# A two-layer backbone kernel on one core: the conditioning vector's silu behind the first tiles, the last tile's root on ScalarE, and another order of all steps

## Chip, cores and metric

The kernel runs on one core of one Trainium2 chip. The metric is device time in microseconds (us), the median over runs; smaller is better. The core has TensorE (PE, matmuls; its weight loads are shown apart as PEld), VectorE (DVE), ScalarE (ACT), GpSimd (POOL) and SyncE (SP), which here only issues transfers (DMA). All data are in fp32; a matmul in the profile works on 128 rows by 256 or 512 columns.

## What is computed

Two layers over 512 latent tokens of width 1024, with 256 context tokens in layer 0. Cut to what matters here:

```python
silu_c = jax.nn.silu(c); silu_cc = jax.nn.silu(c_ctx)
for i in range(2):
    mod_l = silu_c @ ada_w[i] + ada_b[i]                 # six vectors: shifts, scales, gates
    mod_c = silu_cc @ ada_w[i] + ada_b[i]
    h = modulate(rmsnorm(x, norm_g[i, 0]), shift, scale)
    y = mixer(h)                                         # layer 0: windowed attention, layer 1: gated MLP
    x = x + gate * rmsnorm(y, norm_g[i, 1])
    f = swiglu(modulate(rmsnorm(x, norm_g[i, 2]), shift2, scale2), ffn_w_in[i], ffn_w_out[i])
    x = x + gate2 * rmsnorm(f, norm_g[i, 3])
return x
# rmsnorm(y, g) = y * rsqrt(mean(y*y) + 1e-6) * g
```

## The kernel before, in words

**Numbers.** Each fp32 operand is split into a high part, rounded on ACT (`high`, L412, a CAST), and a low part, the difference, on DVE (`low`, L419). A product is then three matmuls: high by high, high by low, low by high. So each slab of weights that comes in costs one CAST and one subtraction before PE may use it whole.

**Order.** The program is a list of steps. `at(time, step, ...)` puts a step on a plan with a due time, but a table of names at the head of the file, `ORDER`, overrides the time: `run_plan` emits the steps in the table's order. Each engine gets its instructions in that order and works them off one by one, waiting at each for what it needs. SP's queue and POOL's queue issue the transfers in the same way. So ORDER decides, for every engine, what stands behind what.

**Start.** The conditioning vector `cc` is loaded by the first transfer, outside the plan; ACT takes its silu (L547) into `sc`, and DVE spreads it into `s4` (L650). Six tiles of tokens (`xin`, four of x and two of ctx) are fetched; for each, ACT takes the mean square (L439), DVE adds the epsilon and POOL raises to -0.5 (`rstd_of`, L448/449), DVE scales (L676), and PE transposes it in two groups of four (`turn_in`, L697). The layer's first modulation vectors come in eight pieces of weights (`ada0`, 1 MB each), which PE multiplies with `s4` (`ada0_rows`, L718) and turns (L729). Then `kv` (L471 to 473) is the first product, over eight slices of the width. `warm` (L684) are matmuls on zeros, to keep PE running while data come. `rope` (L915) turns the tables of the rotary embedding.

**Middle.** Queries and keys are rotated; the last key halves' low parts (`klo`) are needed by the first score (L1099). Later modulation vectors are summed on DVE from chunks and added up over partitions by a matmul with ones (`total`, L612), whose operand is split first (`acc_st`).

**FFN.** For each layer, 22 hidden blocks are formed (L1635), with fewer products by a Strassen-like scheme. The output side is a second such scheme: after the first plain products (`plain7`, L1846, tiles of two banks each) come seven block products (`product7`, L1819), numbered 1 to 7, each in four parts p. Block product i, part p needs the cast weights (`w7_high_i_p`, an ACT CAST), their low part on DVE and cast tokens (`a7_high_i_p`, ACT CAST into `s`). The weights of the blocks (11, 12, 21, 22) are fetched by SP into `w`/`t` tiles (`fetch7_z_h`), and the sums of two blocks are made either on DVE (`t7`, L1801) or by a transfer that POOL issues and that adds in flight (`t7_add`, L1807). Results are saved (`save7`, L1827) and combined (`add7`, L1836).

**End.** In layer 1 the last plain products (`plain7_9`, `plain7_10`) finish the four tiles of the output, y00/y01 for tile 0 to y30/y31 for tile 3. For each tile: `square_y` on ACT for each half (L439), `rstd_y` (DVE L448, POOL L449), `gain_y` on DVE (L1319), `add_x` on DVE (L1323), `store` on SP. Tile 3 is done in halves, each half with its own squares, gains, addition and store. In the old table its second half's matmuls are the very last.

Of the kernel before, what the change touches and what calls it, by code (L numbers as in the profile page):

```python
# [46 lines left out]
ada0_fetch_1 dma#2 ada0_fetch_2 ada0_fetch_4 square_in_2 turn_in_0_0 ada0_rows_out_0 turn_in_0_1 rstd_in_2 norm_in_2_0
norm_in_2_1 ada0_cols_0 turn_in_2_0 whigh_0_0 ada0_rows_1 rope_turned_0 turn_in_2_1 turned_in_0_0 ada0_rows_out_1
turn_in_3_0 <lambda> ada0_done_0 modulate0_ctx_0 ada0_cols_1 wlow_0_0 modulated_ctx_0 kv_0_4 kv_0_5 turned_in_2_0
ada0_done_1 turned_in_3_0 modulate0_0 modulated_high_0 modulated_low_0 wfetch_0_1 modulated_high_1 ada0_rows_2  # L50
ada0_rows_out_2 kv_0_2 turned_in_2_1 modulate0_ctx_1 modulate0_1 modulated_ctx_1 ada0_cols_2 kv_0_1 whigh_0_1 kv_0_0
modulated_low_1 kv_1_4 kv_1_1 kv_1_2 kv_1_5 ada0_done_2 ada0_fetch_3 rope_turned_1 modulate0_ctx_2 turned_in_0_1
modulate0_2 m2start wlow_0_1 modulated_high_2 ada0_rows_4 modulated_ctx_2 ada0_rows_3 ada0_rows_out_4 ada0_cols_4
ada0_done_4 kv_1_0 ada0_rows_out_3 ada0_cols_3 wfetch_1 whigh_1_0 wlow_1_0 whigh_1_1 kv_2_4 modulated_low_2 kv_0_3
ada0_fetch_5 kv_1_3 kv_2_3 kv_2_1 ada0_done_3 modulate0_3 modulated_high_3 modulate0_ctx_3 ada0_rows_5 modulated_ctx_3
kv_3_4 kv_2_5 kv_3_5 modulate0_ctx_4 modulated_ctx_4 modulated_high_4 kv_2_2 kv_4_5 kv_2_0 modulated_low_3
ada0_rows_out_5 ada0_cols_5 kv_3_2 kv_3_3 m2fetch_0 m2add_0 kv_3_0 kv_3_1 dma#3 ada0_fetch_6 ada0_rows_6 m2add_1
modulate0_4 <lambda>#2 ada0_done_5 modulated_high_5 modulate0_ctx_5 ada0_fetch_7 ada0_rows_7 modulated_low_4 kv_4_2
wfetch_2 kv_4_3 ada0_rows_out_6 ada0_cols_6 wlow_1_1 modulate0_5 modulated_low_5 whigh_2_0 wlow_2_0 ada0_done_6
modulate0_6 kv_4_4 ada0_rows_out_7 kv_4_0 m2fetch_1 m2add_2 m2add_3 modulated_high_6 modulated_low_6 kv_5_0 q_first_0_0  # L60
kv_5_3 whigh_2_1 ada0_cols_7 dma#4 modulated_ctx_5 ada0_done_7 modulated_high_7 wlow_2_1 modulate0_ctx_6 kv_4_1 kv_5_1
q_first_0_1 q_first_0_2 q_first_0_3 q_first_0_4 q_first_0_5 kv_5_2 kv_6_3 kv_5_5 modulate0_7 modulated_ctx_6 q_first_0_6
kv_6_0 kv_5_4 m2fetch_2 modulated_low_7 modulate0_ctx_7 kv_7_3 kv_6_1 m2add_4 kv_6_4 m2add_5 m2fetch_3 kv_6_2 kv_7_2
wfetch_3 kv_6_5 kv_7_0 q_first_0_7 kv_7_1 modulated_ctx_7 m2add_6 m2add_7 kv_7_5 kv_7_4 q_first_1_0 table_Exp k_copy_2_0
k_copy_2_1 q_rows_0 v_copy_0 k_copy_0_0 k_rope_2 k_add_2 k_copy_0_1 v_copy_1 k_copy_4_0 k_copy_4_1 v_copy_2 k_rope_0
v_copy_3 q_first_1_1 q_first_1_2 q_first_1_3 q_first_1_4 q_first_1_5 q_first_1_6 q_first_1_7 k_turn_2_1 k_add_0 v_copy_4
# [2167 lines left out]
```

## Time and profile before

| | us |
|---|---|
| median of 3 runs | 1097.65 (1097.63 to 1099.7) |
| the profiled execution | 1098.59 |
| its span | 1096.8 |
| PE busy | 1077.8 |
| DVE busy | 939.1 |
| ACT busy | 601.0 |
| POOL busy | 263.1 |

Rows of the profile give a line of the program, an engine, an operation, and names "out<-in" without their numbers. In a row of waits, "PE y L1819 <- ACT s L412: 1.3, 1, 1.3" means that PE stood idle ahead of a matmul of line 1819 into `y` until ACT's instruction of line 412 on `s` was done, 1.3 us in all, once, at most 1.3. In a timeline, the first two columns are start and duration, and a bracket gives the idle time before and what ended it. In a row of windows come the stretch, its length, the busy time and number of instructions of PE, PEld, DVE, ACT and POOL, PE's granted clock, the share of DMA engines' time and GB/s. The mean granted clock of TensorE was 0.999 of full speed.

### The profile page before, as it was taken

Reading aid. Unit: us, or ns where it says so; the run is one execution under the profiler, and the core shown is the slowest. Engines: PE = TensorE matmul, PEld = TensorE weight load, DVE = VectorE, ACT = ScalarE, POOL = GpSimd, SP = SyncE. Lnnn points to the kernel's source line nnn. Section 1 sums busy time; section 2 is a strip of 40 time slices with the busy share of each in tenths; the row PEclk is TensorE's granted clock in tenths of the full one; section 3 lists DMA queues with packets and bytes.
Section 4 is the critical chain, followed back from the end, with each engine's and each line's share of the span. In section 5 each row is a group of like instructions: output and inputs, shape, how many; then the busy total and the mean of one; then the engine's idle time right before and its main releaser. Section 6 shows DMA issues by size and latency. Waiting matters only on the chain.

```text
span 1096.8 us, 17794 instructions
## 1 busy us (share of the span) xinstructions
PE 1077.8 (98%) x6894; PEld 948.3 (86%) x6894; DVE 939.1 (86%) x1382; ACT 601.0 (55%) x1055; POOL 263.1 (24%) x268
## 2 busy tenths in 40 slices
PE   8999999999999999999899999999999999999997
PEld 5787787878999999998688888888999999998886
DVE  5788998848999999998788878878998888879885
ACT  6456677656554555546565534336655555556662
POOL 1428768426500000003311402006300000003301
PEclk9999999999999999999999999999999999999999
DMA  9745531254245636569942586561233344369911
GB/s 357 285 153 169 179 109 46 78 188 177 77 174 192 212 117 196 170 213 248 238 88 78 203 271 236 192 197 73 96 134 120 113 154 143 113 229 315 172 28 77
DMA packets 50392, 181.25 MB, mean 165 GB/s; under 512 B 5370, under 2 KB 9722, under 8 KB 39172
## 3 DMA queue, kind: packets, MB, share of 16 engines
q1 hardware_dynamic: 42756, 165.44, 43.7%
q0 software_dynamic: 7552, 14.68, 7.9%
q8 instruction: 54, 0.88, 0.3%
q14 instruction: 30, 0.25, 0.1%
HBM read 171.71 MB, written 2.10 MB: 158 GB/s over the span
## 4 chain that ended last, share of the span: by engine, by line
PE 89%; DVE 5%; DMA 3%; issue 1%; ACT 1%; SPq 0%; DVEq 0%; POOLq 0%; POOL 0%; ACTq 0%
PE f L1635 36%; PE y L1819 12%; PE y L479 7%; PE y L1846 6%; PE v L479 4%; PE s_ps L1099 2%; PE pT_ps L1132 2%; PE o_ps L1148 2%; PE q_ps L861 1%; DMA t<-in_w 1%; PE fa L471 1%; PE fa L473 1%; PE fa L472 1%; PE u L2054 1%; PE u L2053 1%; PE u L2052 1%
## 5 line engine op out<-in xcount | busy, mean ns | idle before, releaser
L1635 PE MATMUL f<-H,w_hi 128*128 128x256 f32 x960 | 177.8, 284 | 0.5 <-DVE fc L1646 0.5
L1635 PEld LDWEIGHTS f<-H,w_hi 128*128 128x128 f32 x960 | 150.0, 192 | 1.3 <-DVE fc L1646 1.0
L1635 PE MATMUL f<-H,w_lo 128*128 128x256 f32 x480 | 135.8, 283 | 0.0
L1819 PE MATMUL y<-w_hi,s 128*128 128x512 f32 x448 | 120.6, 390 | 2.5 <-ACT s L412 1.3
L1635 PE MATMUL f<-S,w_hi 128*128 128x256 f32 x640 | 118.5, 284 | 0.5 <-ACT fc L1642 0.5
L412 ACT CAST w_hi<-T 128x1024 fp32r<-128x1024 f32 x80 | 83.7, 1047 | 58.7 <-PE f L1635 41.5
L412 ACT CAST w_hi<-w_raw 128x1024 fp32r<-128x1024 f32 x90 | 94.0, 1054 | 31.1 <-PE f L1635 11.3
L1819 PEld LDWEIGHTS y<-w_hi,s 128*128 128x128 f32 x448 | 83.9, 188 | 20.8 <-DVE s L419 1.8
L419 DVE TENSOR_TENSOR w_lo<-w_raw,w_hi 128x1024 fp32r<-128x1024 f32 (+1 forms) x81 | 96.1, 1192 | 6.4 <-ACT w_hi L412 6.1
L1635 PEld LDWEIGHTS f<-S,w_hi 128*128 128x128 f32 x640 | 99.8, 192 | 0.9 <-ACT fc L1642 0.7
L419 DVE TENSOR_TENSOR w_lo<-T,w_hi 128x1024 fp32r<-128x1024 f32 x80 | 97.3, 1219 | 2.6 <-ACT w_hi L412 2.6
L1635 PEld LDWEIGHTS f<-H,w_lo 128*128 128x128 f32 x480 | 92.1, 192 | 0.0
L1635 PE MATMUL f<-S,w_lo 128*128 128x256 f32 x320 | 90.6, 283 | 0.0
L1642 ACT COPY fc<-f 128x256 f32<-128x256 f32 x120 | 43.6, 372 | 84.2 <-PE f L1635 75.6
L1807 POOL DMA_DIRECT2D t<-in_w x48 | 42.5, 955 | 178.3 <-DMA t<-in_w 105.1
L581 DVE SCALAR_TENSOR_TENSOR acc<-ada_k,sc,acc 128x1024 f32<-128x1024 f32 x56 | 71.6, 1278 | 6.1 <-DMA ada_k<-in_ada 5.7
L595 POOL DMA_DIRECT2D acc<-acc x8 | 6.9, 868 | 286.2 <-DVE acc L581 279.1
L1819 PE MATMUL y<-w_lo,s 128*128 128x512 f32 x224 | 69.3, 391 | 1.1 <-DVE w_lo L419 1.1
L1126 POOL TENSOR_SCALAR p<-p,st 128x512 f32<-128x512 f32 (+1 forms) x64 | 59.8, 948 | 27.5 <-DVE st L1122 14.5
L1635 PE MATMUL f<-H,x 128*128 128x256 f32 x480 | 64.1, 283 | 0.0
L1110 ACT ACTIVATE p<-s_ps,st 128x512 f32<-128x512 f32 (+1 forms) x64 | 47.3, 741 | 25.9 <-DVE st L1105 22.3
L1635 PEld LDWEIGHTS f<-S,w_lo 128*128 128x128 f32 x320 | 61.4, 192 | 0.0
(261 smaller groups left out, 2746.4 us busy)
## 6 DMA issues: line engine op xcount, KB each, us to landing
w_raw<-in_w SPq DMA_DIRECT2D x67, 1024.0 KB, 5.4
ada_k<-in_ada SPq DMA_DIRECT2D x56, 512.0 KB, 5.9
ada_raw<-in_ada SPq DMA_DIRECT2D x12, 1024.0 KB, 5.4
w<-in_w SPq DMA_DIRECT2D x12, 1024.0 KB, 7.6
t<-in_w POOLq DMA_DIRECT2D x48, 256.0 KB, 6.3
ada<-in_ada SPq DMA_DIRECT2D x8, 1024.0 KB, 8.4
t<-in_w SPq DMA_DIRECT2D x8, 1024.0 KB, 10.7
w_raw<-in_w SPq DMA_DIRECT2D x10, 512.0 KB, 7.3
```

The lines of the kernel that those rows point to most:

```text
L412: nc.scalar.copy(out=hi, in_=src)
L419: (eng or nc.vector).tensor_tensor(out=v(lo), in0=v(src), in1=v(hi).bitcast(F32), op=ALU.subtract)
L479: nc.tensor.matmul(dst, l, w[:, n * 512:(n + 1) * 512], start=first and i == 0, stop=last and i == 2)
L581: nc.vector.scalar_tensor_tensor(out=self.acc, in0=self.raws.pop(k), scalar=sc[:, k:k + 1], in1=self.acc, op0=ALU.mult, op1=ALU.add)
L1099: nc.tensor.matmul(dst, q, keys, start=i == 0, stop=i == 1)
L1110: nc.scalar.activation(out=p[:, 0:self.n], in_=self.s[j], func=AF.Exp, scale=-1.0, bias=self.st[:, 4 + j:5 + j], accum_out=self.st[:, 8 + ...
L1126: nc.gpsimd.tensor_scalar(out=p, in0=p, scalar1=self.st[:, 12 + j:13 + j], scalar2=1.0, op0=ALU.mult, op1=ALU.mult)
L1635: nc.tensor.matmul(dst, l[:, w], r[:, k, :], start=first and k == 0 and j == 0, stop=k == 3 and j == 2, skip_group_check=True)
L1642: nc.scalar.copy(out=self.c[n][:, i * 256:(i + 1) * 256], in_=self.ps[n, 1 if i == 1 else 0])
L1807: nc.gpsimd.dma_start(out=self.tt[:, p * D + 512 * i:p * D + 512 * (i + 1)], in_=a["w"][F2[self.layer] + 1 + 2 * p + i][:, c:c + 512], acc ...
L1819: nc.tensor.matmul(self.bank7(i, j), st[:, c:c + P], w[:, z * 512:(z + 1) * 512], start=i == 1 and p == 0 and l == 0 and z == 0, stop=p == ...
L1846: nc.tensor.matmul(self.y[t][n], st[:, x + t * P:x + (t + 1) * P], parts[h][w][:, n * 512:(n + 1) * 512], start=v == 0 and h == 0 and i == ...
```

## The change

Three things. First, the transfer of `cc`, its silu and its spread become steps `cc_in`, `cc_silu` and `cc_spread` of the plan, and the table sets their places. Second, in the last stage the tile that is done in halves (tile 3) gets its inverse root otherwise: DVE adds the epsilon to the first half's mean square (`bias_y`), ACT takes the root of the second half's with that as its bias (`root_y`, Sqrt) and DVE inverts (`invert_y`); the root's table is loaded ahead, by `table("Sqrt")`, and `table` now takes minus the constant as its operand so that a root of it exists. Third, ORDER is another list throughout; of its old and new names only those steps differ.

```diff
-x_fetch_1 square_in_1 rstd_in_1 norm_in_1_0 rope_in warm_0 warm_1 warm_2 warm_3 norm_in_1_1 x_fetch_4 square_in_4
+rope_in dma rope_turn_0 rope_turned_0 x_fetch_3 warm_0 warm_1 warm_2 warm_3 square_in_3 rstd_in_3 warm_4 norm_in_3_1
...
     def table(func):
-        nc.scalar.activation(out=tabled, in_=mhalf, func=getattr(AF, func))
+        nc.scalar.activation(out=tabled, in_=mhalf, func=getattr(AF, func), scale=-1.0)
...
-    dma(cc, a["cc"])
...
-    nc.scalar.activation(out=sc, in_=cc, func=AF.Silu)
...
-    for z in range(2):
-        nc.vector.tensor_copy(out=s4[:, :, 2 * z], in_=sc[:, z * KC:(z + 1) * KC])
+    def cc_in():
+        dma(cc, a["cc"])
+    def cc_silu():
+        nc.scalar.activation(out=sc, in_=cc, func=AF.Silu)
+    def cc_spread():
+        for z in range(2):
+            nc.vector.tensor_copy(out=s4[:, :, 2 * z], in_=sc[:, z * KC:(z + 1) * KC])
...
     at(0, x_fetch, 0)
+    at(.1, cc_in)
+    at(4, cc_silu)
+    at(4.2, cc_spread)
...
+        def bias_y(self):
+            self.b = small(1, "by")
+            nc.vector.tensor_scalar(out=self.b, in0=self.ms[0], scalar1=RMS_EPS, scalar2=None, op0=ALU.add)
+        def root_y(self):
+            self.r = small(1, "ry")
+            nc.scalar.activation(out=self.r, in_=self.ms[1], func=AF.Sqrt, bias=self.b)
+        def invert_y(self):
+            nc.vector.reciprocal(out=self.r, in_=self.r)
...
-                at(e + .15, c.rstd_y)
+                at(e + .05, c.bias_y)
+                at(e + .12, c.root_y)
+                at(e + .15, c.invert_y)
+            at(b, table, "Sqrt")
```

**Start.** ACT's instructions at the program's head, before (`sc<-cc` is the silu; `xin` are the tiles, in the order in which they are taken: x1, ctx4, x3, ctx5, x0):

```order
L551 ACT_TABLE_LOAD
L551 CAST ones_73<-ones32_71 128x128
L547 ACT_TABLE_LOAD
L547 ACTIVATE sc_69<-cc_61 128x16
L439 ACTIVATE junk_108,ms0_107<-xin_105 128x1024
L439 ACTIVATE junk_125,ms0_124<-xin_122 128x1024
L439 ACTIVATE junk_135,ms0_134<-xin_132 128x1024
L703 COPY xnT0_97<-xT_141 128x4x128
L439 ACTIVATE junk_168,ms0_167<-xin_146 128x1024
```

and after (the tiles are x3, ctx5, x1, ctx4, x0):

```order
L551 ACT_TABLE_LOAD
L551 CAST ones_71<-ones32_69 128x128
L930 COPY ropeT_83<-rope_104 128x512
L441 ACTIVATE junk_130,ms0_129<-xin_122 128x1024
L441 ACTIVATE junk_150,ms0_149<-xin_147 128x1024
L654 ACT_TABLE_LOAD
L654 ACTIVATE sc_68<-cc_61 128x16
L441 ACTIVATE junk_165,ms0_164<-xin_162 128x1024
L441 ACTIVATE junk_187,ms0_186<-xin_184 128x1024
```

The silu and its table load have moved from ahead of all tiles to behind the squares of two of them. On SP the order of fetches has changed with it: rope, ident, x3, cc, ctx5, x1, cols, ctx4, x0, x2, and then the first piece of `ada0`; x2 came behind that piece before. On PE all twelve groups of transposes now stand ahead of the `rows` of the second piece; two stood behind it.

**Layer 0's seven products.** ACT's instructions around the weights of product 2, parts 2 and 3, before (`w_hi_5909` and `w_hi_5914` are the weights of product 7, parts 3 and 2, `w_hi_5920` and `w_hi_5926` those of product 2, parts 3 and 2; `s7_5929` are the tokens of 2_2):

```order
L412 CAST w_hi_5909<-t7_5724 128x1024
L412 CAST s7_5912<-act4_5055 128x512
L412 CAST w_hi_5914<-t7_5724 128x1024
L412 CAST s7_5918<-act4_4430 128x512
L412 CAST w_hi_5920<-t7_5724 128x1024
L412 CAST w_hi_5926<-t7_5724 128x1024
L412 CAST s7_5929<-act4_4430 128x512
```

and after (`w_hi_5948` and `w_hi_5953` are product 7, parts 2 and 3, `w_hi_5958` and `w_hi_5978` product 2, parts 2 and 3; `s7_5951` are the tokens of 2_2, `s7_5975` those of 2_3):

```order
L414 CAST w_hi_5948<-t7_5694 128x1024
L414 CAST s7_5951<-act4_4447 128x512
L414 CAST w_hi_5953<-t7_5694 128x1024
L414 CAST w_hi_5958<-t7_5694 128x1024
L414 CAST s7_5975<-act4_4976 128x512
L414 CAST w_hi_5978<-t7_5694 128x1024
```

The tokens of 2_2 now come ahead of its weights, and its weights ahead of those of 2_3. On SP the fetch of these weights (`fetch7_21_1`) keeps its place behind `fetch7_22_0_raw`, which waits for the step `t7_3` of DVE as before. On PE product 2_2 is still the eleventh of the parts. In layer 1 the table moves `f1fetch7_12_1_raw` from ahead of blocks 12, 21 and 22 to behind both halves of 22, and the sums `f1t7_2` and `f1t7_3` that need it to just ahead of product 5.

**End.** ACT's last instructions before (y31 is the second half of tile 3, y10 and y11 are tile 1):

```order
L439 ACTIVATE junk_11194,msy_11193<-y01_10503 128x512
L439 ACTIVATE junk_11197,msy_11196<-y00_10502 128x512
L439 ACTIVATE junk_11212,msy_11211<-y20_10433 128x512
L439 ACTIVATE junk_11227,msy_11226<-y21_10434 128x512
L439 ACTIVATE junk_11254,msy_11253<-y30_10468 128x512
L439 ACTIVATE junk_11270,msy_11269<-y10_10527 128x512
L439 ACTIVATE junk_11273,msy_11272<-y11_10528 128x512
L439 ACTIVATE junk_11297,msy_11296<-y31_10469 128x512
```

and after:

```order
L441 ACTIVATE junk_11196,msy_11195<-y30_10518 128x512
L441 ACTIVATE junk_11205,msy_11204<-y31_10519 128x512
L1332 ACTIVATE ry_11211<-msy_11204,by_11209 128x1
L441 ACTIVATE junk_11234,msy_11233<-y20_10488 128x512
L441 ACTIVATE junk_11237,msy_11236<-y21_10489 128x512
L441 ACTIVATE junk_11255,msy_11254<-y01_10470 128x512
L441 ACTIVATE junk_11258,msy_11257<-y00_10469 128x512
L441 ACTIVATE junk_11295,msy_11294<-y10_10453 128x512
L441 ACTIVATE junk_11301,msy_11300<-y11_10454 128x512
```

Tile 3, with the root on ACT (L1332), now comes first of the four, and tile 1 last; PE's last 24 matmuls are those of y10 and y11 in turn, where the last 12 were those of y31 alone. The last two stores are whole tiles of 512 KB, where they were halves of 256 KB. DVE's sum `add7_c12_1` into y11, which PE's last matmuls need, stands behind the gains, the inversion and an addition of tile 3 and the gains of tile 2.

More of the change, by code (lines that the diff above doesn't have):

```diff
@@ L47 @@
[L47 to L66, printed above, removed]
@@ new lines @@
+c1turned_hi_0 c3merge c2rstd_x c3square_y c3gain_y c3rstd_y f0part_high_2_0 c1turned_lo_0 f0first_half_1#2
+f0part_low_2_0 c3add_x c3gain_x c2shift_x_1 f0head_0_2 c1turned_hi_1 f0head_1_0 c1turned_lo_1 c3square_x c2turn_1
+c3rstd_x f0part_high_3_0 c2shift_x_0 c2turned_hi_1 m5start c3shift_x_0 f0head_1_1 f0diff_2_1 f0first_half_0
+f0part_high_2_2 m5fetch_chunk_1_spare m0fetch_gain c2turn_0 c3shift_x_1 c2turned_hi_0 c2turned_lo_0 f0diff_2_3
+f0diff_2_2 f0part_low_3_0 f0sum_a_S3 f0product_2_1 c2turned_lo_1 c3turn_1 f0part_low_2_2 f0sum_a_S2 f0first_half_0#2
@@ new lines @@
+f0keep_12_2 f0product_13_1 f0up2_11 f0keep_12_1 f0part_high_13_1 f0part_high_13_2 m0fetch_chunk_3_spare f0gate1_11
+f0silu_11_0 f0keep_13_0 f0product_12_3 f0product_11_4 f0silu_11_1 f0gate1_12 m0add_chunk_2 f0part_low_13_1
+f0part_low_13_2 f0gates_11 m5stack f0part_high_14_0 f0part_high_14_2 f0product_13_5 f0diff_14_1 f0part_low_14_0
+wfetch_25 f0product_12_7 f0up2_12 m1fetch_chunk_0_spare f0part_high_13_3 f0diff_14_3 f0diff_14_2 f0part_low_13_3
+f0product_13_6 f0keep_13_1 f0product_13_2 f0product_12_4 f0keep_13_2 f0product_13_7 f0up1_12 m5total_0_slot
@@ new lines @@
+f0plain7_0_2 f0plain7_0_3 f0t7_2 f0save7_v0_0 f0save7_v0_1 f0a7_high_1_0 f0gates_21 m1total_0_slot f0a7_high_2_1
+m1done_512 m1done_0 f0w7_low_1_0 f0w7_high_1_1 f0a7_low_2_1 f0fetch7_12_1 f0s7_S3_1 f0fetch7_21_0 f0a7_low_1_0
+f0w7_low_1_1 f0a7_high_1_1 f0a7_low_1_1 f0plain7_0_1 f0a7_high_1_2 f0w7_high_1_2 f0t7_add_1_22 f0plain7_0_0
+f0a7_high_1_3 f0w7_high_2_1 f0w7_low_1_2 f0w7_high_2_0 f0a7_high_2_0 f0a7_low_1_2 f0product7_1_0 f0a7_high_7_1
+f0product7_1_1 f0t7_add_0_22 f0t7_0 f0w7_low_2_0 f0product7_1_2 f0a7_low_1_3 f0w7_high_7_0 f0s7_S3_2 f0t7_3
@@ new lines @@
+whigh_48_1 m4fetch_chunk_1 wlow_47_1 u_part_0_1 v_part_3_(3,) v1rstd v0mean wlow_48_1 wlow_48_0 m4fetch_chunk_2
+m4add_chunk_1 m4add_chunk_2 table_Gelu v0var v0rstd v0gain v1gain m4fetch_chunk_5 v0bias v3add v1bias wfetch_49
+whigh_49_0 u_part_1_0 m4fetch_chunk_4 m2mirror#2 m4add_chunk_3 v3gelu v3mean v2add v3var whigh_49_1 wfetch_50
+m4add_chunk_4 wlow_49_0 m4add_chunk_5 v2gelu v2mean v2var m4fetch_chunk_7 u_part_1_1 m4fetch_chunk_6 wlow_49_1
+u_part_2_0 whigh_50_0 whigh_50_1 wlow_50_1 m3fetch_chunk_0 ws_in wfetch_51 m3start#2 bias_in m2stack#2 v2rstd
@@ new lines @@
+f1keep_16_2 f1part_high_17_0 f1part_low_17_0 f1diff_17_3 f1diff_17_2 f1part_high_17_2 gains f1part_low_17_2
+f1product_16_2 f1product_16_7 f1up2_16 f1silu_13_1 f1product_17_1 f1product_16_3 f1keep_17_0 f1part_high_17_1 f1gates_13
+f1product_15_7 f1product_17_2 f1diff_18_1 f1diff_17_4 wfetch_74 f1part_high_18_0 f1up2_15 f1silu_15_0 f1product_15_4
+f1silu_15_1 f1product_16_4 m5add_chunk_5#2 f1part_high_17_3 f1part_low_17_1 f1up1_16 f1product_17_5 f1keep_17_1
+f1s7_S3_2 f1gate1_17 f1gate1_16 f1product_17_6 f1silu_16_0 f1diff_18_3 f1diff_18_2 f1diff_18_4 f1part_high_18_2
@@ L395 @@
+c2add_x#4 c0gain_y_0_512 c0gain_y_512_1024 f1plain7_9_1 c0rstd_y#4 c0add_x#4 c0store f1plain7_10_1 c3add_x_0_512
+c1square_y_0_512 c1gain_y_0_512 c3store_0_512 c1square_y_512_1024 c1rstd_y#4 c1gain_y_512_1024 c2store c1add_x#4 c1store
 """.split()
```

659 lines of the change are left out of this document (327 added, 332 removed).

## The prediction

> **What bounds the kernel now.** I read the page first, for the share of each engine.
>
> ```profile
> PE 1077.8 (98%) x6894; PEld 948.3 (86%) x6894; DVE 939.1 (86%) x1382; ACT 601.0 (55%) x1055; POOL 263.1 (24%) x268
> ```
>
> TensorE (PE) is busy for 1077.8 of 1096.8 us. The change adds and removes no matmul, so all that it can win lies in the 19.0 us in which PE does nothing. The waits of PE say what these are:
>
> ```profile
> PE warm L684 <- DVE idle L681: 1.8, 1, 1.8
> PE xT L697 <- DVE r L446: 1.6, 1, 1.6
> PE y L1819 <- ACT s L412: 1.3, 1, 1.3
> PE s_ps L1099 <- DVE klo L419: 1.2, 1, 1.2
> PE y L1819 <- DVE s L419: 1.2, 1, 1.2
> PE xT L697 <- DVE xin L676: 1.2, 2, 0.7
> PE y L1819 <- DVE w_lo L419: 1.1, 1, 1.1
> PE s_ps L1099 <- ACT p L1110: 1.0, 2, 0.7
> PE f L1635 <- DVE fc L1646: 0.5, 1, 0.5
> PE f L1635 <- ACT fc L1642: 0.5, 1, 0.5
> ```
>
> The rows of L684 and L697 (1.8, 1.6 and 1.2) lie ahead of the first product and cost nothing by themselves, as the chain of the first 24 us shows:
>
> ```profile
> 2.13 5.61 DMA xin<-in_ctx
> 7.74 0.02 issue
> 7.76 12.80 DMA ada<-in_ada
> 20.69 1.07 PE rows L718 x16
> 21.76 1.02 PE xT L697 x8
> ```
>
> There transfers set the pace, and PE begins the `rows` of the second piece of the modulation weights at 20.69, when that piece is in. From then on PE hardly stops before its last matmul. The rest of the idle time is in three places: four waits of about 1.2 us each from the list above, smaller ones, and the end after the last matmul. So I look at the start, at those waits, and at the end, each against the new order of its engine.
>
> **The start.** The change puts the load of `cc` fourth on SyncE's queue, and Silu with its table load behind two tiles' squares on ScalarE (ACT). What these cost ACT is in its timeline:
>
> ```profile
> 2.35 1.28 ACT L547 ACT_TABLE_LOAD   x1
> 3.64 0.22 ACT L547 ACTIVATE sc<-cc 128x16 f32<-128x16 f32 x1
> 5.01 1.06 ACT L439 ACTIVATE junk<-xin 128x1024 bf16<-128x1024 f32 x1 [1.15 <-DMA xin<-in_x]
> 7.83 1.06 ACT L439 ACTIVATE junk<-xin 128x1024 bf16<-128x1024 f32 x1 [1.67 <-DMA xin<-in_ctx]
> 16.55 1.07 ACT L439 ACTIVATE junk<-xin 128x1024 bf16<-128x1024 f32 x1
> ```
>
> Before, load and Silu (1.28 + 0.22 = 1.50 us) lay in the time ACT waits for its first tile, which came in at 5.0. After, they stand between squares, while ACT waited 1.67 for the third tile anyway; so the 1.5 us have a cover of 1.15 + 1.67 in all, and I put them at nothing. If that cover is gone (the tiles come closer together), they delay all later squares by up to 1.5. The last tile's square was at 16.55 because the tile came late; in the new order of fetches this tile comes ahead of the first piece of weights. Two of the twelve groups of transposes stood behind `rows` before: the row "21.76 1.02 PE xT L697 x8". In the new order of PE all twelve groups precede that `rows`, and the bytes queued ahead of the second piece are the same, so it lands as before. The first product then begins one group of transposes earlier: **-1.0 us**. Bounds: -1.6 if PE's earlier wait on `r` (1.6) vanishes as well and shifts the pieces, +0.5 if the 1.5 us of load and Silu hit with 1.0 saved. I take -1.0, the row itself.
>
> [...]
>
> **The first scores (83 us).** PE waits 1.2 for `klo` once. DVE's timeline has the subtractions for it:
>
> ```profile
> 83.06 1.28 DVE L419 TENSOR_TENSOR klo<-kT,khi 128x512 fp32r<-128x512 f32 x2
> ```
>
> The first score reads what the second of the two writes. In the new order the two have changed places, and one takes 1.28 / 2 = 0.64, so **-0.6**; bounds 0 and -1.2, the whole wait.
>
> **The modulation totals (485 to 488 us).** PE's timeline:
>
> ```profile
> 487.75 0.50 PE L612 MATMUL ada_ps<-acc_st,ones 128*128 128x512 f32 x1 [0.28 <-ACT acc_st L412]
> 488.48 0.50 PE L612 MATMUL ada_ps<-acc_st,ones 128*128 128x512 f32 x1 [0.23 <-DVE acc_st L419]
> ```
>
> With the wait of `f` on `fc` (0.5) just ahead, these are 0.28 + 0.23 + 0.5 = 1.0 us. The new order takes the first total earlier, among the products of the last hidden block, and the second later, inside the plain product; both operands have then been cast for long. I take **-0.8**, between 0 and -1.0.
>
> **The seven products of layer 0 (533 to 541 us).** ACT's timeline and PE's:
>
> ```profile
> 532.24 1.99 ACT L412 CAST w_hi<-t 128x1024 fp32r<-128x1024 f32 x2 [8.02 <-DMA t<-in_w]
> 534.14 1.13 ACT L412 CAST s<-act 128x512 fp32r<-128x512 f32 x2
> ```
>
> ```profile
> 534.81 0.73 PE L1819 MATMUL y<-w_hi,s 128*128 128x512 f32 x2 [1.32 <-ACT s L412]
> 536.67 0.74 PE L1819 MATMUL y<-w_lo,s 128*128 128x512 f32 x2 [1.13 <-DVE w_lo L419]
> 541.35 0.50 PE L1819 MATMUL y<-w_hi,s 128*128 128x512 f32 x1 [1.17 <-DVE s L419]
> ```
>
> ACT stands 8.02 us at a cast whose weights are not yet in, with the cast of the tokens `s` behind it. When they come, at 532.2, it does two weight casts (1.99) before that `s` (1.13 for two), and PE, whose queue has run dry, loses 1.32 + 1.13 + 1.17 = 3.6. The fetch stands at the same place in SyncE's queue after, behind the same step of DVE, so I let it land at the same time. But ACT's order is another: the tokens of product 2_2 are cast ahead of the wait, and the weights of 2_2 ahead of those of 2_3. Left over is then one weight cast and one subtraction for its low part, which PE sees as one wait like that of 1.13 (1.2 with a margin): 3.6 - 1.2 = **-2.4**. Bounds: 0 if the other pieces come in later and the wait only changes its name, -3.6 if all goes.
>
> **The end.** Here the change of the last tile's root lies. The old end:
>
> ```profile
> 1087.67 0.39 PE L1846 MATMUL y<-w_lo,st 128*128 128x512 f32 x1
> 1089.94 0.39 PE L1846 MATMUL y<-w_hi,st 128*128 128x512 f32 x1
> ```
>
> ```profile
> 1090.42 0.60 ACT L439 ACTIVATE junk<-y 128x512 bf16<-128x512 f32 x1 [1.54 <-PE y L1846]
> ```
>
> ```profile
> 1088.92 0.22 DVE L448 TENSOR_SCALAR ry<-msy 128x1 f32<-128x1 f32 x1
> 1089.83 1.28 DVE L1323 SCALAR_TENSOR_TENSOR x<-tmp,ry,x 128x1024 f32<-128x1024 f32 x1
> 1092.02 1.41 DVE L1323 SCALAR_TENSOR_TENSOR x<-tmp,ry,x 128x512 f32<-128x512 f32 x2
> ```
>
> ```profile
> 1091.44 0.55 POOL L449 TENSOR_TENSOR ry<-ry,mhalf 128x1 f32<-128x1 f32 x1 [1.68 <-DVE ry L448]
> ```
>
> PE ends at 1089.94 + 0.39 = 1090.33. One square, the addition of the epsilon, the power on GpSimd (POOL, 0.55) and two half additions (1.41) follow, until 1092.02 + 1.41 = 1093.43, that is 3.10 after PE; the last store holds 256 KB, since the first half left ahead of it. Sending the root to ACT shortens this chain by the way to POOL and back, if this tile is the last. But in the new order of PE the split tile, tile 3, with the new root, is the first of the four to end; tiles 2 and 0 follow, and the last 24 matmuls are those of tile 1, on two banks in turn, with the old chain. What that costs is shown by tile 1 in the old run: its last matmul lay 12 matmuls ahead of the end, at the pace of (1089.94 - 1087.67) / 10 = 0.227 us, so at 1090.33 - 2.73 = 1087.60; its addition ended at 1089.83 + 1.28 = 1091.11, 3.51 after it, since two squares follow each other instead of one. That is +0.4 against 3.10. Its store is one of 512 KB:
>
> ```profile
> 12.00:20.00 8.00, 6.42 (x56) 4.93 (x57) 6.34 (x15) 5.82 (x12) 2.72 (x4) 1.00 1.02 417
> ```
>
> At the 417 GB/s that the DMA engines moved in this window when full, 256 KB more take 0.6. Together +1.0 us, and I add 0.2, since the sum that DVE must write into `y11` ahead of its last matmuls now stands behind the gains and the first half addition of tile 3: **+1.2**. Bounds +0.6 (stores overlap fully but for half of the second square) and +1.9 (PE waits a whole 0.69 addition more). So the new root itself, 0.55 us of power taken away, wins nothing at the end: no engine waits for it there. Its table load lies in a stretch in which ACT is idle for half of the time:
>
> ```profile
> 1040.00:1085.00 45.00, 45.00 (x199) 36.77 (x198) 34.60 (x46) 21.12 (x32) 4.36 (x5) 1.00 0.16 30
> ```
>
> ACT is busy 21.12 of 45.00 us there, so 1.28 are free; if it hit just when PE needs a cast, it would cost up to 1.28.
>
> **What the rest of the order brings.** Every engine's order differs nearly everywhere, and the trace can't show the waits that it makes. The list above is what an order leaves between 23 and 1090 us: ten or so waits, from 0.5 to 1.3. I allow **+0.7** for new ones, between 0 and 3.6, the largest cluster that the old order left.
>
> **Sum.** -1.0 - 0.6 - 0.8 - 2.4 + 1.2 + 0.7 = -2.9. The profiled run took 1098.59 us (span 1096.8), so it would be 1095.7 there; the median of the runs before is 1097.65, 0.94 lower, which makes 1094.8. A measurement can tell some 0.2% (2.2 us) of this kernel from no change, so "faster" begins below 1095.45 and "slower" above 1099.85.
>
> **Rivals.** *The wait in layer 0 keeps its size.* PE's wait at 533 to 541 is at bottom a transfer that lands at 532; if weights land no earlier and 2_2 is as late by its low part and the next tokens, the -2.4 falls away: -2.9 + 2.4 = -0.5, 1097.15. For it speaks that the fetch stands where it stood; against it that the first of the three waits is on `s`, which is now cast ahead. Chance 0.27.
>
> *Slower: the same stall comes again in layer 1.* There the new order fetches the second half of block 12 last, behind both halves of block 22, and DVE's sums of it with block 11 stand directly ahead of product 5 that uses them. If that transfer lands after PE's queue of product 3 has run dry, ACT stands at the cast as in the row of 8.02 and PE loses another 3.6, while layer 0 keeps its own: -0.5 + 3.6 = +3.1, 1100.75. It decides when the transfer lands later than PE's products 1, 7, 2, 6 and 3 last. Against it: PE had no such wait in layer 1 before, and the DMA share is low there (0.16 in the window above). Chance 0.15.
>
> *The Silu becomes the bound of the start.* If the tiles come in close together, the 1.50 us lie on the chain of squares and the start gives +0.5 instead of -1.0: -2.9 + 1.5 = -1.4, 1096.25. Chance 0.10. [...]
>
> *The new order is better than I can see.* All four gains at their bounds (-1.6 - 1.2 - 1.0 - 3.6), the end at +1.0 and no new waits: -6.4, 1091.25. Chance 0.10.
>
> That the change does nothing of what its name says for the last tile is not a rival but part of the forecast: by the order it isn't last.
>
> **How the numbers follow.** The forecast has 0.38, and by its unknown waits reaches from 1093 to 1096.5; of this 0.31 is faster and 0.07 the same. The better order adds 0.10 to faster, the kept wait 0.03 faster, 0.21 same, 0.03 slower, the Silu 0.02 faster and 0.08 same, the stall in layer 1 0.15 slower. Faster 0.46, same 0.36, slower 0.18. The range from 1091.0 to 1100.5 takes in forecast and both cases of no change, and cuts the two ends about in the middle.
>
> **What would show it.** Right: the first product begins near 21.7 to 22; PE's waits on `s` at 533 to 541 shrink to one of about 1.2; PE ends about 4 us earlier against the span's start than 1090.33, and the span ends 7.4 to 7.7 after PE instead of 6.5, with a 512 KB store last. Wrong: a wait of PE above 2 us at a new place, a first product later than 23, or a tail of 6 us or less.

## The result and the profile after

The changed kernel is slower: 1101.18 us in the median of 8 runs (1099.49 to 1102.26) beside 1097.82 for the kernel before (8 runs, the three of the table above among them, 1097.63 to 1099.7); ratio 1.0028, 95% interval 1.0018 to 1.0037. 1094.8 was forecast. Its profiled run took 1101.11, span 1099.3, that is 2.5 us more than the 1096.8 of before.

The first row of the page, and all rows of the waits of PE that the changed kernel has:

```profile
PE 1078.4 (98%) x6894; PEld 950.6 (86%) x6894; DVE 941.6 (86%) x1383; ACT 601.9 (55%) x1058; POOL 264.7 (24%) x267
```

```profile
PE q_ps L872 <- DVE klo L421: 7.5, 1, 7.5
PE rope L926 <- DMA ident<-in_ident: 3.6, 1, 3.6
PE s_ps L1110 <- ACT p L1121: 2.0, 3, 1.0
PE pT_ps L1143 <- ACT pt L1150: 0.2, 1, 0.2
```

Read against the list of before: every wait on which the prediction put a gain is gone, those of `y` (1.3, 1.2 and 1.1), of `f` (0.5 and 0.5), of `ada_ps` (0.3 and 0.2) and that of the first score on `klo`. The scores wait longer for `p` (2.0 instead of 1.0); the wait of `rope` lies ahead of the `warm` matmuls and costs nothing by itself. In place of those that are gone stands one of 7.5 us, which the list of before has not: PE's third query product, `q_ps`, waits for a subtraction of keys on DVE, with which it shares no operand. PE's and DVE's timelines at that place:

```profile
73.32 2.78 PE L1030 MATMUL kT<-ident,kr 128*128 128x128 f32 x24
83.58 1.22 PE L872 MATMUL q_ps<-HA,w_hi 128*128 128x512 f32 x2 [7.47 <-DVE klo L421]
84.60 0.63 PE L872 MATMUL q_ps<-HA,w_lo 128*128 128x512 f32 x1
...
87.56 0.63 PE L872 MATMUL q_ps<-HA,w_hi 128*128 128x512 f32 x2
...
91.00 0.39 PE L1110 MATMUL s_ps<-khi,q_X 128*128 128x512 f32 x1
```

```profile
76.13 1.28 DVE L421 TENSOR_TENSOR klo<-kT,khi 128x512 fp32r<-128x512 f32 x2
81.04 1.28 DVE L421 TENSOR_TENSOR klo<-kT,khi 128x512 fp32r<-128x512 f32 x2
82.84 1.28 DVE L421 TENSOR_TENSOR klo<-kT,khi 128x512 fp32r<-128x512 f32 x2
```

The product begins at 83.58, when the first subtraction of the third pair has ended (82.84 + 0.64 = 83.48). In the kernel before, the same product followed the transposes at once. PE's rows and one of DVE's:

```profile
74.74 2.78 PE L1019 MATMUL kT<-ident,kr 128*128 128x128 f32 x24
77.56 0.73 PE L861 MATMUL q_ps<-HA,w_hi 128*128 128x512 f32 x2
78.13 0.39 PE L861 MATMUL q_ps<-HA,w_lo 128*128 128x512 f32 x1
...
84.49 0.47 PE L1099 MATMUL s_ps<-khi,q_X 128*128 128x512 f32 x1 [1.19 <-DVE klo L419]
```

```profile
76.83 0.68 DVE L419 TENSOR_TENSOR klo<-kT,khi 128x512 fp32r<-128x512 f32 x1
```

There is a second loss in these rows. After the pause the 24 matmuls of the product take 91.00 - 83.58 = 7.42 us; at 0.227 each they would take 5.45. The first nine come 0.44 apart ((87.56 - 83.58) / 9), the rest 0.23. The pause so costs 7.5 and another 2.0. The granted clock shows the second part: it is half from 80.69, within the pause, until 87.51 (rows of windows):

```profile
80.69:84.10 3.41, 0.52 (x1) 0.50 (x2) 3.41 (x6) 1.12 (x2) 1.95 (x3) 0.50 0.62 154
84.10:87.51 3.41, 3.41 (x9) 2.64 (x8) 1.39 (x3) 0.11 (x1) 0.00 (x0) 0.50 0.00 0
87.51:90.92 3.41, 3.41 (x16) 2.77 (x15) 0.00 (x0) 0.00 (x0) 0.00 (x0) 1.00 0.00 0
```

The end of the changed kernel, on PE and DVE:

```profile
1091.24 0.61 PE L1868 MATMUL y<-w_hi,st 128*128 128x512 f32 x2
```

```profile
1092.45 0.69 DVE L1341 TENSOR_TENSOR tmp<-y,row 128x512 f32<-128x512 f32 x1 [0.46 <-ACT junk L441]
1093.17 0.22 DVE L450 TENSOR_SCALAR ry<-msy 128x1 f32<-128x1 f32 x1
1094.09 1.28 DVE L1345 SCALAR_TENSOR_TENSOR x<-tmp,ry,x 128x1024 f32<-128x1024 f32 x1
```

PE ends at 1091.24 + 0.61 = 1091.85, and the span 7.4 after it, where it was 6.5. The last addition ends at 1094.09 + 1.28 = 1095.37, that is 3.5 after PE.

So the 2.5 us split like this, from one landmark of PE to the next (the first transposes of keys, the first score, the last matmul, the end). Up to the transposes 73.32 against 74.74: -1.4. From there to the first score 17.68 against 9.75: +7.9. From there to PE's end 1000.85 against 1005.84: -5.0. The end: +1.0.

### The profile page after: what moved, and what is told of

Its sections match the earlier page's. It is cut to its first block, busy times and chain, and to the rows that moved or that the text cites. A ratio compares the mean times of both kernels' runs of the same rounds, so it can differ in the third digit from the quotient of the medians.

```text
span 1099.3 us, 17847 instructions
## 1 busy us (share of the span) xinstructions
PE 1078.4 (98%) x6894; PEld 950.6 (86%) x6894; DVE 941.6 (86%) x1383; ACT 601.9 (55%) x1058; POOL 264.7 (24%) x267
## 4 chain that ended last, share of the span: by engine, by line
PE 90%; DVE 4%; DMA 1%; POOL 1%; issue 1%; ACT 1%; SPq 0%; DVEq 0%; ACTq 0%; POOLq 0%
PE f L1657 37%; PE y L1841 14%; PE y L481 7%; PE y L1868 6%; PE v L481 4%; PE o_ps L1159 3%; PE s_ps L1110 3%; PE pT_ps L1143 2%; PE q_ps L872 2%; PE fa L475 1%; PE fa L473 1%; PE fa L474 1%; PE u L2079 1%; PE u L2078 1%; PE u L2077 1%; POOL w_lo L421 1%
## 5 line engine op out<-in xcount | busy, mean ns | idle before, releaser
L1137 POOL TENSOR_SCALAR p<-p,st 128x512 f32<-128x512 f32 (+1 forms) x64 | 56.0, 907 | 34.0 <-DVE st L1133 26.1
L1116 DVE CUSTOM_DVE_ANT_0 s_ps<-s_ps,mask,nsink 128x512 f32<-128x512 f32 (+1 forms) x64 | 51.3, 820 | 14.8 <-PE s_ps L1110 13.7
```

The source lines that it names most:

```text
L1116: nc.vector.tensor_tensor_reduce(out=s, in0=s, in1=self.msk, scale=-1.0, scalar=nsink[:, h:h + 1], op0=ALU.add, op1=ALU.min, accum_out=sel ...
L1137: nc.gpsimd.tensor_scalar(out=p, in0=p, scalar1=self.st[:, 12 + j:13 + j], scalar2=1.0, op0=ALU.mult, op1=ALU.mult)
```

## The experiments

**Why the product waits.** The kernel puts PE's sums into tiles in PSUM, which it hands out in banks; the pool that holds the transposed keys has eight. `q_ps` has a bank of its own, in a pool that takes over the banks when the pool of the keys is closed. So its bank has held other data, and e1 (a wait of 7.47 us gone) and e2 (one of 3.49 made) show that the product begins only when the last reader of those is done. The built programs name the bank of each. `kT (t,g)` are the transposed keys of tile pair t, half g of the heads:

```
          in the order in which they are transposed                               q_ps   first score
before    (2,1): 5   (4,1): 2   (4,0): 6   (0,0): 1   (0,1): 3   (2,0): 0         5      0 and 1
after     (4,0): 6   (2,1): 3   (4,1): 0   (0,1): 7   (0,0): 5   (2,0): 1         5      0 and 1
subtractions on DVE, before:  (2,1)   (0,1)   (4,0) (4,1)   (2,0) (0,0)
subtractions on DVE, after:   (2,1) (4,1)   (0,1) (4,0)   (0,0) (2,0)
```

`q_ps` lies in bank 5 in both. Before, this bank held the keys that are split first (from 76.83 to 77.51, and the product began at 77.56, so it just fitted); after, those that are split last but one (at 82.84). Theory A says that this alone makes the wait; theory B, that the product waits for its operands or for DVE's queue as such.

*e1_q_bank4*: the changed kernel with `q_ps` in bank 4, which held the second query product and is copied out at 74. (`o_ps` takes bank 5 for it; its first matmul is at 105.8.)

```diff
+    psR_p.tile([P, 512], F32, name="q_ps", tag="q", bufs=1)
     psR_p.tile([P, 512], F32, name="o_ps", tag="o", bufs=1)
```

> The changed kernel, only with the query product's accumulator in another PSUM bank (4, that of the query rows copied out at 74 us, instead of 5). Theory A (bank): in the changed kernel the product of the third query pair waited 7.47 us at 76.1 us because its bank still held the transposed keys of tile 0, first half, whose low part VectorE subtracts only at 82.84. Then this wait goes, the product starts at about 76.2, ends at 81.6 at 0.227 us a matmul, and the first score then waits about 2.6 us for the last key subtraction (84.1); first score at 84.2 instead of 91.0, time 1101.2 - 6.8 = 1094.4. Theory B (operands): the product waits for its own operands or for VectorE's queue as such; then nothing moves, 1101.2.

Measured: 1093.13 (4 runs, 1092.56 to 1095.25), 8.0 below the changed kernel; ratio to the kernel before 0.996 (0.9946 to 0.9975). PE:

```profile
73.69 2.78 PE L1030 MATMUL kT<-ident,kr 128*128 128x128 f32 x24
76.23 0.70 PE L872 MATMUL q_ps<-HA,w_hi 128*128 128x512 f32 x2
...
84.42 0.50 PE L1111 MATMUL s_ps<-khi,q_X 128*128 128x512 f32 x1 [2.46 <-DVE klo L421]
...
86.72 0.63 PE L872 MATMUL q_ps<-HA,w_lo 128*128 128x512 f32 x1
```

and DVE's last pair of subtractions:

```profile
83.08 1.28 DVE L421 TENSOR_TENSOR klo<-kT,khi 128x512 fp32r<-128x512 f32 x2
```

The product stands behind the transposes without a pause, and no order of any engine was changed for it: theory A. The gain is larger than expected since the runs other than the profiled one came out 2.0 to 2.7 below it. Their mean granted clock was 0.998 to 0.999 beside its 0.996, so the slow pace behind the first score was probably shorter or missing in them, which is not shown. What is left is the 2.46 at the first score: it begins when the last subtraction, that of (2,0), has ended (83.08 + 1.28 = 84.36), and one of its two banks held those keys.

*e2_before_bank6*: the kernel before, with `q_ps` in the bank of the keys (4,0).

```diff
+    psR_p.tile([P, 512], F32, name="pT_ps", tag="pT", bufs=2)
+    psR_p.tile([P, 512], F32, name="q_ps", tag="q", bufs=1)
     psR_p.tile([P, 512], F32, name="o_ps", tag="o", bufs=1)
```

> The kernel before, only with the query product's accumulator in bank 6, which there holds the keys of tile 4, first half (in the kernel before it is bank 5, whose keys are the first to be split). Theory A: the wait appears in the kernel before: the product stands from 77.5 until the subtraction of those keys ends, the second of the pair at 81.18, so 81.9: 4.3 us; the old wait of 1.2 ahead of the first score goes, and if TensorE's clock is low after this pause, up to 1.9 more: 1097.8 + 3.1 to + 5.0, 1100.9 to 1102.8. Theory B: 1097.8.

Measured: 1102.85 (4 runs, 1101.4 to 1103.28), 4.8 above the kernel before (1098.03 in the runs beside it); ratio 1.0047 (1.003 to 1.0063). PE and DVE:

```profile
80.53 1.19 PE L861 MATMUL q_ps<-HA,w_hi 128*128 128x512 f32 x2 [3.49 <-DVE klo L419]
81.52 0.63 PE L861 MATMUL q_ps<-HA,w_lo 128*128 128x512 f32 x1
```

```profile
79.70 1.28 DVE L419 TENSOR_TENSOR klo<-kT,khi 128x512 fp32r<-128x512 f32 x2
```

The same wait, in the kernel that had none, by two lines that reserve banks. It is 3.49 and not 4.3, since (4,0) is the first of its pair and DVE was 1.5 us earlier there. With e1 this settles the cause.

*e3_fill*: the changed kernel, PE kept at work during the pause.

```diff
     run_plan()
+    filled = bankA("fill")
+    for i in range(32):
+        nc.tensor.matmul(filled, HA[:, 0, 0:P], HA[:, 0, :], start=True, stop=True)
     psA.__exit__(None, None, None)
```

> The changed kernel with 32 matmuls of no use (their result is not read) put on TensorE ahead of the waiting product, 32 x 0.227 = 7.3 us, in a bank that is free. Theory of the clock: after the pause of 7.47 us the next nine matmuls took 0.43 instead of 0.227, 1.9 us lost, because TensorE had stood still; kept busy it loses only the wait, so 1101.2 - 1.9 = 1099.3, with the product at 83.6 and the first score at 89.1. Rival: the slow pace has to do with these matmuls' data or bank; then 1101.2.

Measured: 1098.87 (10 runs, 1098.44 to 1101.44), 2.3 below the changed kernel. The matmuls write to bank 4, which is free. PE:

```profile
75.85 7.54 PE L1070 MATMUL fill<-HA 128*128 128x512 f32 x32
83.23 0.62 PE L872 MATMUL q_ps<-HA,w_hi 128*128 128x512 f32 x2
...
88.67 0.39 PE L1113 MATMUL s_ps<-khi,q_X 128*128 128x512 f32 x1
```

The product begins behind the last of the added matmuls, 0.35 earlier than in the changed kernel, and takes 88.67 - 83.23 = 5.44 instead of 7.42; together these are the 2.3. The slow pace comes from the standing still, not from the bank or the data. So of the changed kernel's loss 2.0 us are TensorE's clock; the mean granted clock of the profiled run is 0.999 here beside 0.995 there. In the changed kernel the clock is half from 4.6 us after PE's last matmul ahead of the pause to 3.9 us after the first one behind it (76.10, 80.69, 83.58 and 87.51). A pause as long as that is not needed: single matmuls took 0.63 behind pauses of 2.46 us in e1 and 1.85 in e5 too. The last section sets the pauses side by side.

**The end.** *e4_split_last*: e1, and the last steps of the table in the order of before, with tile 3 last and its root on ScalarE.

```diff
-... f1plain7_10_3_(0,) c3square_y_0_512 f1plain7_10_3_(1,) ... f1plain7_10_2 ... f1plain7_10_0 ... f1plain7_10_1 ... c1store
+... f1plain7_10_0 ... f1plain7_10_2 ... f1plain7_10_1 ... c1store f1plain7_9_3_(1,) f1plain7_10_3_(1,) c3square_y_512_1024
+c3root_y c3gain_y_512_1024 c3invert_y c3add_x_0_512 c3store_0_512 c3add_x_512_1024 c3store_512_1024
```

> As the first kernel of this call, and the last steps in the old order, with the halved tile 3 last, but with its root on ScalarE. Theory of the end: the changed kernel's end was 1.2 us longer because tile 1, with two squares and a 512 KB store, ended last; with tile 3 last again that goes, and the root on ScalarE (about 0.3 of square root and 0.2 of reciprocal against 0.22 + 0.55) gives 0.2 to 0.5 more: 1.4 to 1.7 below the first kernel of this call, about 1092.9. Rival: the end is set by the stores alone; then equal to the first kernel.

Measured: 1092.9 (4 runs, 1091.29 to 1093.39), 0.2 below e1, less than the runs scatter. So the time does not show the gain that was expected. Its profile, of the fastest of the four runs (span 1089.5), has the end as expected; PE, ScalarE and VectorE:

```profile
1082.69 0.39 PE L1874 MATMUL y<-w_hi,st 128*128 128x512 f32 x1
```

```profile
1083.17 0.60 ACT L446 ACTIVATE junk<-y 128x512 bf16<-128x512 f32 x1 [1.54 <-PE y L1874]
1083.67 0.20 ACT L446 ACTIVATION_READ_ACCUMULATOR junk<-y 128x1 f32 x1
1083.89 0.29 ACT L1338 ACTIVATE ry<-msy,by 128x1 f32<-128x1 f32 x1
```

```profile
1083.90 0.69 DVE L1347 TENSOR_TENSOR tmp<-y,row 128x512 f32<-128x512 f32 x1
1084.50 0.15 DVE L1341 RECIPROCAL ry<-ry 128x1 f32<-128x1 f32 x1
1084.69 1.41 DVE L1351 SCALAR_TENSOR_TENSOR x<-tmp,ry,x 128x512 f32<-128x512 f32 x2
```

The span ends 1089.5 - 1083.08 = 6.4 after PE, 1.0 less than the changed kernel. From the end of the square to the addition it takes 1084.69 - 1083.87 = 0.82; with POOL it took 0.91 (1092.02 - 1091.11). The root on ScalarE takes 0.29, but the product with the gain (0.69) now sets the time.

*e7_root_only*: the kernel before in its old order, with the steps of the root exchanged alone.

```diff
-... c3square_y_512_1024 c3rstd_y#4 c3gain_y_512_1024 ...
+... c3bias_y c3square_y_512_1024 c3root_y c3gain_y_512_1024 c3invert_y ...
```

> The kernel before in its old order, with one part of the change alone: the last tile's root on ScalarE (its table load behind the last hidden block's silu), inverted on VectorE. In the order of before this tile is the last. The old chain from the end of the square to the first addition took 0.91 us (0.22 + 0.55 and the ways), the new one in e4 0.82, since VectorE's product with the gain now stands in it: 0.1 less, 1097.9 beside 1098.0, no difference that can be measured. Rival: the ways between the engines count and the root on ScalarE gives the 0.5 us of POOL's power: 1097.5; by a switch of tables that stalls ScalarE for long, slower.

Measured: 1097.88 (11 runs, 1096.63 to 1099.17) beside 1098.04; ratio 0.9996 (0.9987 to 1.0005). Nothing that can be measured, with this tile the last; the table load stands behind the last hidden block's silu, at 983.

**The pause at the first score.** *e5_split_early*: e1, and the subtractions moved ahead of the next pair's rotation.

```diff
-... q_swap_1 q_cos_1 k_split_0_1 v_copy_5 q_sin_1 k_split_4_0 q_add_1 k_split_0_0 k_turn_2_0 k_split_2_0 ...
+... q_swap_1 k_split_0_1 v_copy_5 k_split_4_0 k_split_0_0 k_turn_2_0 k_split_2_0 q_cos_1 q_sin_1 q_add_1 ...
```

> As e1_q_bank4, and the last four subtractions of the keys' low parts on VectorE ahead of the next query pair's rotation (its product with the cosines and the addition, 0.69 each), not between and behind them. In e1 TensorE waited 2.46 us ahead of the first score for the last of them and then did some ten matmuls at 0.43 instead of 0.227, so 2.0 more. Theory: the last subtraction ends 1.3 earlier, the pause is 1.2 to 1.4, and if such a short pause leaves the clock alone, the gain against e1 is 1.2 + 2.0 = 3.2: 1090 (if the clock falls all the same, 1092). Rival: the second query pair, now later by 1.3 to 2.6, makes the third score wait instead: 1093.

Measured: 1094.31 (5 runs, 1093.85 to 1094.69), 1.2 above e1, whose runs overlap with these: not the gain, but the rival in another form. The score no longer waits; the next product does. PE and ScalarE:

```profile
84.28 0.73 PE L877 MATMUL q_ps<-HA,w_hi 128*128 128x512 f32 x2 [1.85 <-ACT q_rot L957]
...
86.20 1.06 PE L877 MATMUL q_ps<-HA,w_hi 128*128 128x512 f32 x2
```

```profile
82.35 1.25 ACT L419 CAST q_X<-q_rot 64x512 fp32r<-64x512 f32 x2 [3.46 <-DVE q_rot L975]
83.63 0.60 ACT L957 ACTIVATE q_rot<-q_ps 128x512 f32<-128x512 f32 x1
```

ScalarE stands 3.46 us at a cast of the second query pair, which waits for VectorE's addition, now later; behind it in its queue is the copy that frees `q_ps`.

*e6_early_last*: e5 with the end of e4.

```diff
-... c3store_0_512 c1square_y_512_1024 c1rstd_y#4 c1gain_y_512_1024 c2store c1add_x#4 c1store
+... c3square_y_512_1024 c3root_y c3gain_y_512_1024 c3invert_y c3add_x_0_512 c3store_0_512 c3add_x_512_1024 c3store_512_1024
```

> As e5_split_early, with the halved tile 3 last again, as in e4_split_last. Theory of the end: the span ends 6.4 us after the last matmul instead of 7.5, so 1.1 below e5_split_early, about 1089. Rival: as e4 and e1 lay 0.2 apart in the median, the order of the tiles is worth nothing: equal to e5.

Measured: 1093.7 (5 runs, 1092.81 to 1095.67), 0.6 below e5 with ranges that overlap.

*e9_rows_first*: e6, with the table's entries of that cast behind the copy.

```diff
-... q_add_1 q_high_1_0 q_low_1_0 q_high_1_1 q_low_1_1 q_step_2_0 ... q_rows_2 score_0_0 ...
+... q_add_1 q_step_2_0 ... q_rows_2 q_high_1_0 q_low_1_0 q_high_1_1 q_low_1_1 score_0_0 ...
```

> As e6_early_last, and on ScalarE the copy of the third query pair out of its bank (q_rows_2) ahead of the casts of the second pair (q_high_1), behind which it stood. In e5 TensorE waited 1.85 us for that copy, since ScalarE stood 3.46 us at the casts' wait for VectorE, and then did ten matmuls at 0.43, 2.0 more. Theory: no pause of a microsecond is left on TensorE between 76 and 90 us; 3.5 to 3.9 below e6 (1093.7), about 1090. Rival: the second pair, later again, makes a later score wait: no gain, 1093.

Measured: 1093.12 (5 runs, 1092.64 to 1095.44). The edit changed no instruction: the casts belong to an earlier plan than the copy, and the table orders steps only within one `run_plan`. So the expectation was not tried, and e9 is e6 a second time, with the same 2.0 us of wait for the copy.

*e12_tile1_last*: the same edit on e5, so e5 a second time.

```diff
-... q_add_1 q_high_1_0 q_low_1_0 q_high_1_1 q_low_1_1 q_step_2_0 ...
+... q_rows_2 q_high_1_0 q_low_1_0 q_high_1_1 q_low_1_1 score_0_0 ...
```

> As e9_rows_first, but with the end in the changed kernel's order: tile 3 first, tile 1 last. Theory of the end: the span ends 7.4 us after the last matmul instead of 6.4, so 0.7 to 1.1 above e9. Rival: equal to e9.

Measured: 1094.8 (7 runs, 1093.28 to 1096.49). Its profile has a wait at the score (1.0) and one at the next product (2.1). Put together, tile 1 last (e5 and e12, 12 runs) has a median of 1094.35, tile 3 last with its root on ScalarE (e6 and e9, 10 runs) 1093.51: 0.8 apart, with ranges that overlap. That is the sign and nearly the size that the spans of 7.4 and 6.4 after PE give, but the mean granted clock of the two groups differs as well, 0.997 against 0.998, and 0.001 of 1093 us is 1.1. So the order of the tiles is seen in the profiles, behind PE's end, and not in these medians.

**The waits of layer 0.** *e8_act_order*: the kernel before, with the order of ScalarE alone.

```diff
-... f0a7_high_7_2 f0w7_high_2_3 f0a7_low_7_2 f0s7_S2_2 f0a7_low_7_3 f0w7_high_2_2 f0a7_high_2_2 ...
+... f0a7_high_7_2 f0a7_high_2_2 f0w7_high_2_2 f0w7_high_2_3 f0a7_low_7_2 f0s7_S2_2 f0a7_low_7_3 ...
```

> The kernel before, with ScalarE's casts around the wait in layer 0's seven products in the order of the changed kernel: the tokens of 2_2 ahead of the wait, then the weights of 2_2, then those of 2_3. Theory C (the prediction's): the transfer lands as before, at 532, and of the 3.6 us of waits one of about 1.2 is left: 1098.0 - 2.4 = 1095.6. Theory D: the wait went in the changed kernel since the transfer took 10 us and not 15, with fewer of POOL's adding transfers beside it; then the order of ScalarE alone gives 1 us or less: 1097 to 1098.

Measured: 1096.54 (10 runs, 1096.0 to 1099.68), 1.5 below; ratio 0.9989 (0.998 to 0.9998). PE's waits there and ScalarE's:

```profile
PE y L1825 <- DVE s L425: 0.9, 1, 0.9
PE y L1825 <- ACT s L418: 0.6, 1, 0.6
...
PE y L1825 <- DVE w_lo L425: 0.5, 2, 0.3
```

```profile
531.25 2.00 ACT L418 CAST w_hi<-t 128x1024 fp32r<-128x1024 f32 x2 [6.09 <-DMA t<-in_w]
```

3.6 us of waits became 2.0, not 1.2. The transfer still comes at 531, and ScalarE waits 6 us for it. The result lies between the two theories.

*e11_fetch_ahead*: the kernel before, with that fetch ahead of the one which held it back.

```diff
-... f0a7_low_1_2 f0fetch7_22_0_raw ...
+... f0a7_low_1_2 f0fetch7_21_1 f0fetch7_22_0_raw ...
```

> The kernel before with one edit: in layer 0's seven products SyncE fetches the second half of block 21 ahead of block 22's first half, which waits for a sum of VectorE at 515.7 and held it back until 517.4. Theory D: the waits of TensorE at 533 to 541 hang on when that transfer lands; issued some 18 us earlier it has landed before the cast, and all of 3.6 to 4.1 us go: about 1094.1. Theory C: the waits come from the order on ScalarE, and the landing matters little: 1096 to 1098.

Measured: 1095.68 (11 runs, 1094.34 to 1098.05), 2.7 below the kernel before, 1098.36 in the runs beside it; ratio 0.9977 (0.9968 to 0.9986). Its profiled run is the slowest of the eleven (1098.05), so the profile shows less of the gain than the median. ScalarE's wait is shorter and at another cast of weights:

```profile
524.13 1.05 ACT L418 CAST w_hi<-t 128x1024 fp32r<-128x1024 f32 x1 [3.82 <-DMA t<-in_w]
```

and PE has 2.0 us of waits left there (1.3 on `s`, 0.5 on `w_lo`, 0.2 on `w_hi`). Neither the order alone (1.5) nor the landing alone (2.7) takes away all: each leaves 2.0 of the 3.6 us of waits. The changed kernel has the new order and a quicker transfer, and there ScalarE waited for PE and not for a transfer:

```profile
531.78 0.62 ACT L414 CAST s<-act 128x512 fp32r<-128x512 f32 x1 [1.49 <-PE y L1841]
532.30 2.00 ACT L414 CAST w_hi<-t 128x1024 fp32r<-128x1024 f32 x2
```

The fetch was issued at 522.93 and landed at 532.92, 10.0 us later, where the same fetch took 14.8 before (517.38 to 532.14). In the first 6 us of the old one POOL issued three transfers that add in flight (two at 518.48, and one at 521.67); beside the new one it was a single one, at 522.48, just ahead of it. That these slowed the old one is argued from the times, not tried.

**The start.** *e10_cc_first*: e6 with the three steps of `cc` at the head.

```diff
-rope_in dma rope_turn_0 ...
+cc_in cc_silu cc_spread rope_in dma rope_turn_0 ...
```

> As e9_rows_first, but the load of cc, its silu and its spread at the head of all steps, as in the kernel before. Theory: the start's gain in the changed kernel (keys' transposes begin at 73.3 instead of 74.7) comes from the order of fetches and transposes, and the place of cc is worth nothing: equal to e9 within 0.5. Rival: the gain comes from the place of cc: 1.0 to 1.4 above e9.

Measured: 1094.31 (5 runs, 1093.42 to 1094.89) beside 1093.51 of e6 and e9. The transposes of keys begin at 73.90; in the profiles of the eight kernels with the start of the changed one they begin between 72.88 and 73.69. So 0.8 of the start's gain against 74.74 stays without moving `cc`; whether its place gives the last 0.2 to 1.0 stays open at this scatter, and the time, 0.8 above, falls between the two theories.

## Why the prediction was wrong

**The first scores: the step that failed.** It gave -0.6, since the subtraction that the first score needs stands one place ahead. That looked at one reader of the keys, the score, and at the order of one engine. It did not ask who else waits for a subtraction: the next accumulator in the same bank. The change permuted the six transposes and what took banks ahead of them (the six get 5, 2, 6, 1, 3 and 0 in the old order, and 6, 3, 0, 7, 5 and 1 in the new), and the subtractions too; so bank 5 went from the first subtraction to the last but one. Measured: +7.9 at the first score, 7.5 of wait and 2.0 of slow clock, less the old wait and what else lay there. e1 takes it away without an order, e2 makes it in the old kernel, e3 splits it. The term for new waits, +0.7 and at most 3.6, had no room for it, since it went by the waits that the old order had left; the prediction's own sign of being wrong, a wait of PE above 2 us at a new place, is what came.

The -0.6 itself would not have come either. In e1, without that wait, the first score still waits for the second subtraction of the last pair, now (2,0). It does not read these keys (it reads those of tiles 0, 1, 4 and 5) but takes their bank, 1. In the old kernel its banks 0 and 1 held both of the last pair. That the bank is the reason here is read from the table; no run moved the score's banks.

**The start:** forecast -1.0, measured -1.4 at the transposes of keys. The first `kv` came at 21.38 instead of 22.76: the `rows` of the second piece began at 20.38, 0.3 earlier, and one group of transposes fewer lay behind them, the 1.0 of the forecast. That the table load between the tiles' squares cost nothing was right, but not for the reason given. Its cover was to be ScalarE's wait for the third tile; that tile's transfer had ended at 8.94, and its square began 1.4 later, behind load and silu:

```profile
8.91 1.28 ACT L654 ACT_TABLE_LOAD   x1
10.20 0.22 ACT L654 ACTIVATE sc<-cc 128x16 f32<-128x16 f32 x1
10.32 1.04 ACT L441 ACTIVATE junk<-xin 128x1024 bf16<-128x1024 f32 x1
```

So the rival's condition, tiles that come close together, held, and still nothing was lost: PE was at `warm` and `rope` until its first transposes of a tile, and has no wait for a tile in its list. The load takes 1.28 us, as in the kernel before, and the silu stands 0.01 behind it. That this term came out is in part luck.

**Totals, layer 0 and new waits:** forecast -0.8, -2.4 and +0.7 with 0.2 of the tail term inside PE's time, -2.3 in all; measured -5.0 between the first score and PE's end. The waits of 485 to 488 (-1.5) and of 533 to 541 (-3.6) are gone altogether, the scores' wait for `p` grew by 1.0, and PE is busy for 0.9 less there (998.5 against 999.4). The direction was right, the sizes too small: of `f` the sum had one wait of 0.5 and not both, and in layer 0 the transfer also took 10.0 us instead of 14.8, which the prediction took as unchanged.

**The end:** forecast +1.2, measured +1.0 behind PE, and by the parts that were named: the last addition ends 3.5 after PE (3.51 was said, 3.10 it was), and the span 3.9 after the addition instead of 3.4 (+0.6 was said). That the root would win nothing since its tile is not last was right, and e7 shows that it wins nothing measurable where it is last either.

**The slower rival** named 1100.75, close to what came, by another mechanism: a late transfer in layer 1. PE has no wait for that in the changed kernel's list. The number was near by chance.

Without the one step the change would have been faster, and by more than the forecast of 2.9: the other parts make -1.4 - 5.0 + 1.0 = -5.4. e1, which has all of the change without that wait, lies 4.9 below the kernel before in the median; its profiled run, the slowest of its four, lies 3.3 below in the span (1093.5 against 1096.8), with the pause at the score and the slow pace behind it. e1, e4 and e6 are faster than both kernels.

## What to carry to other kernels

An order of steps also hands out buffers: before a permutation is priced, list for each new accumulator which earlier tile had its bank and who reads that tile last. Where the releaser of a wait shares no operand with the waiting instruction, look for a buffer: here it was one (7.47 us, gone in e1), and reserving another bank is a one-line test. A pause of TensorE is priced with the slow pace that may follow it: here 2.0 us lost behind the 7.47 of the changed kernel and 1.6 behind the 1.85 of e5, but nothing behind the 1.99 of e9. Where PE stands still anyway, matmuls of no use can fill the pause: in e3 that was worth 2.3 us.
